# Row maxima of an 8192 x 8192 matrix: first tile in four strided loads, last row by DVE transposes, results in six stores, pieces recut

One core of one Trainium2 chip. The metric is the device time of one execution in microseconds (us), lower is better.

## The reference

```python
x = np.random.randn(8192, 8192).astype(np.float32)
def reference(x):
    return np.linalg.norm(x, ord=np.inf, axis=1)      # max |x| of each row
```

268.4 MB are read and 32 KB are written. 128 rows make a tile, one row to a partition; there are 64 such "rows" of tiles.

## The kernel before

SyncE issues all loads into a ring buffer, most of them for two rows of tiles at once (a double tile). VectorE (DVE) reduces each piece; where a row was cut, a short reduce, called the combine below, puts its partial maxima together. TensorE (PE) and ScalarE (ACT) turn the results round so that each row of results is contiguous, and ACT issues their stores. The last row of tiles is handled apart: its pieces are reduced into columns behind the last piece, and one final reduce takes piece and columns together.

```python
PIECES = (
    [[8192]] * HEAD                       # HEAD = 4
    + [[16384]] * 23                      # two rows of x per partition
    + [[8192, 8192], [7232, 9152], [6720, 9664], [8640, 7744], [5568, 5568, 5248]]
    + [[4480, 3712], [3392, 1920, 2880], [2752, 1600, 2048, 1792]]
    + [[1792, 1664, 1472, 1280, 1088, 896]]
)
RING = 3 * 16384
CUT = 48              # rows below CUT go straight into res, the others through part
...
    fin = single.tile([P, 1], FP32)
...
    def pairs_out():                      # 56 of the 64 rows of results
        ...
        nc.scalar.dma_start(
            out=out[: X_ONE * P].rearrange("(g p r) -> g p r", p=P, r=2), in_=sb)
...
            nc.sync.dma_start(out=buf, in_=src[:, off : off + w])
            if final:
                absmax(fin[:, :1], last)
                break
...
        if u == len(PIECES) - 2:          # all but the last row are reduced
            nc.vector.tensor_reduce(out=res[:, CUT:], in_=part, ...)
            pairs_out()
            singles_out()

    fin_ps = psum_pool.tile([1, P], FP32)
    fin_sb = single.tile([1, P], FP32)
    nc.tensor.transpose(fin_ps, fin, ident)
    nc.vector.tensor_copy(out=fin_sb, in_=fin_ps)
    nc.sync.dma_start(out=out[(R - 1) * P :].rearrange("(r p) -> r p", p=P), in_=fin_sb)
```

No wait is written by hand. The framework adds them, and gives each load and store on SyncE's and ACT's queues one of eight completion semaphores in turn: the issue records name 100, 101 and 103 to 108, seven times each. A semaphore is a counter that a transfer raises as it lands; the seven loads on 100 raised it 112 times.

Of the kernel before, what the change touches and what calls it, by code (L numbers as in the profile page):

```python
# [1 line left out]

# [5 lines left out]

P = 128
FP32 = mybir.dt.float32  # L10
MAX = mybir.AluOpType.max




HEAD = 4
PAIRS = 28
PIECES = (
    [[8192]] * HEAD
    + [[16384]] * 23  # L20
    + [[8192, 8192], [7232, 9152], [6720, 9664], [8640, 7744], [5568, 5568, 5248]]
    + [[4480, 3712], [3392, 1920, 2880], [2752, 1600, 2048, 1792]]
    + [[1792, 1664, 1472, 1280, 1088, 896]]
)
RING = 3 * 16384


CUT = 48
K = 4


@with_exitstack
def kernel(
    ctx: ExitStack,
    tc: tile.TileContext,
    x: bass.AP,
    out: bass.AP,
):
    nc = tc.nc
    n_rows, n_cols = x.shape  # L40
    R = n_rows // P
    assert R == 64 and n_cols == 8192

    X_ONE = 2 * PAIRS

    single = ctx.enter_context(tc.tile_pool(name="single", bufs=1))
    psum_pool = ctx.enter_context(tc.tile_pool(name="psum", bufs=1, space=bass.MemoryType.PSUM))

    ring = single.tile([P, RING], FP32)
    res = single.tile([P, R - 1], FP32)  # L50
    part = single.tile([P, R - 1 - CUT, K], FP32)
    nc.gpsimd.memset(part, 0.0)  # L52
    ident = single.tile([P, P], FP32)
    make_identity(nc, ident)


    n_last = len(PIECES[-1]) - 1
    w_last = PIECES[-1][-1]
    last = single.tile([P, w_last + n_last], FP32)
    fin = single.tile([P, 1], FP32)  # L60

    def absmax(dst, src):
        nc.vector.tensor_reduce(  # L63
            out=dst, in_=src, axis=mybir.AxisListType.X, op=MAX, apply_absolute_value=True,
        )

    def singles_out():
        n = R - 1 - X_ONE
        ps = psum_pool.tile([n, P], FP32, name="ps_singles")
        sb = single.tile([n, P], FP32, name="sb_singles")  # L70
        nc.tensor.transpose(ps, res[:, X_ONE:], ident)  # L71
        nc.scalar.copy(sb, ps)  # L72
        nc.scalar.dma_start(
            out=out[X_ONE * P : (R - 1) * P].rearrange("(r p) -> r p", p=P), in_=sb
        )

    def pairs_out():
        sb = single.tile([PAIRS, P, 2], FP32, name="sb_pairs")
        both = res[:, :X_ONE].rearrange("p (g r) -> p g r", r=2)
        for r in range(2):  # L80
            ps = psum_pool.tile([PAIRS, P], FP32, name=f"ps_pairs{r}")
            nc.tensor.transpose(ps, both[:, :, r], ident)  # L82
            nc.scalar.copy(sb[:, :, r], ps)  # L83
        nc.scalar.dma_start(
            out=out[: X_ONE * P].rearrange("(g p r) -> g p r", p=P, r=2), in_=sb
        )

    at = 0
    next_pair, next_one = 0, X_ONE
    for u, widths in enumerate(PIECES):  # L90
        k = sum(widths) // n_cols
        if k == 2:
            row, next_pair = next_pair, next_pair + 2
        else:
            row, next_one = next_one, next_one + 1
        src = x[row * P : (row + k) * P].rearrange("(p r) m -> p (r m)", r=k)
        off = 0
        n_part = {}
        for h, w in enumerate(widths):
            final = u == len(PIECES) - 1 and h == n_last  # L100
            if final:
                buf = last[:, :w]
            else:
                if at + w > RING:
                    at = 0
                buf = ring[:, at : at + w]
                at += w
            nc.sync.dma_start(out=buf, in_=src[:, off : off + w])  # L108
            if final:
                absmax(fin[:, :1], last)  # L110
                break
            s = 0
            while s < w:
                r = row + (off + s) // n_cols
                left = n_cols - (off + s) % n_cols
                c = (w - s) // n_cols if left == n_cols else 0
                if c and r + c <= CUT:
                    absmax(
                        res[:, r : r + c],
                        buf[:, s : s + c * n_cols].rearrange("p (c m) -> p c m", m=n_cols),  # L120
                    )
                    s += c * n_cols
                    continue
                e = min(w, s + left)
                i = n_part.get(r, 0)
                n_part[r] = i + 1
                if r == R - 1:
                    absmax(last[:, w_last + i : w_last + i + 1], buf[:, s:e])
                else:
                    absmax(part[:, r - CUT, i : i + 1], buf[:, s:e])  # L130
                s = e
            off += w
        if u == len(PIECES) - 2:
            nc.vector.tensor_reduce(  # L134
                out=res[:, CUT:], in_=part, axis=mybir.AxisListType.X, op=MAX,
            )
            pairs_out()
            singles_out()

    fin_ps = psum_pool.tile([1, P], FP32)  # L140
    fin_sb = single.tile([1, P], FP32)
    nc.tensor.transpose(fin_ps, fin, ident)  # L142
    nc.vector.tensor_copy(out=fin_sb, in_=fin_ps)  # L143
    nc.sync.dma_start(out=out[(R - 1) * P :].rearrange("(r p) -> r p", p=P), in_=fin_sb)


# [1 line left out]
_INS = ['x']  # L148
_OUTS = [((8192,), 'float32')]


# [23 lines left out]
```

## Time and profile before

| | before |
|---|---|
| median of 3 runs | 630.57 us (630.52 to 630.62) |
| span of the profiled run | 629.1 us |
| first reduce on DVE starts | 13.30 us |
| last wait of DVE for a load ends | 487.50 us |
| final reduce ends | 626.36 us |

The profile's main views are read in the prediction below. One line more: the waits of DVE for loads. Its columns are the total in us, the number of waits, and the longest. The longest wait is the one for the first tile.

```profile
DVE part L63 <- DMA ring<-in_x_dram: 16.3, 4, 13.3
```

And from the page's groups, the two instructions that bring the last row into one partition (busy us, mean ns of one | idle time before them and what ended it):

```profile
L143 DVE COPY fin_sb<-fin_ps 1x128 f32<-1x128 f32 x1 | 0.3, 279 | 0.5 <-PE fin_ps L142 0.5
...
L142 PE MATMUL fin_ps<-ident,fin 128*1 128x128 f32 x1 | 0.4, 373 | 8.1 <-DVE fin L63 8.1
```

### The profile page before, as it was taken

The page shows a single profiled execution, that of the slowest core. Times are in us where ns is not written, and L with a number is a line of the kernel's source. Part 1 is how long each engine was busy: PE and PEld are TensorE (multiplying, and loading weights), DVE is VectorE, ACT ScalarE, POOL GpSimd, SP SyncE. Part 2 cuts the span into 40 slices and gives each one's busy share as a digit, 9 for nine tenths or more (in the row PEclk, how much of TensorE's full clock was granted, in tenths as well). Part 3 has the DMA queues.
Part 4 walks back from the last instruction along what each step waited for, and adds up shares of the span by engine and source line. Part 5 has one row for each costly group of instructions (what it writes and reads, how often), then busy time and mean ns, then how long its engine had stood idle before and what let it go on. Part 6 is the DMA issues. An engine that isn't in the chain of part 4 may idle for free.

```text
span 629.1 us, 217 instructions
## 1 busy us (share of the span) xinstructions
PE 1.2 (0%) x4; PEld 0.3 (0%) x4; DVE 552.6 (88%) x59; ACT 2.0 (0%) x4; POOL 0.8 (0%) x7
## 2 busy tenths in 40 slices
PE   0000000000000000000000000000000000000000
PEld 0000000000000000000000000000000000000000
DVE  1983988889988889888898888998888999999998
ACT  0000000000000000000000000000000000000000
POOL 0000000000000000000000000000000000000000
DMA  8999999999999999999999999999999999999996
GB/s 367 433 467 404 463 404 463 400 467 404 463 404 463 404 463 404 463 404 463 404 463 404 463 408 458 408 458 408 458 408 429 431 447 432 427 426 424 425 423 265
DMA packets 7692, 268.49 MB, mean 427 GB/s; under 512 B 870, under 2 KB 906, under 8 KB 2058
## 3 DMA queue, kind: packets, MB, share of 16 engines
q1 hardware_dynamic: 7634, 268.44, 99.0%
q10 hardware_dynamic: 56, 0.03, 0.0%
q14 instruction: 2, 0.02, 0.0%
HBM read 268.44 MB, written 0.03 MB: 427 GB/s over the span
## 4 chain that ended last, share of the span: by engine, by line
DMA 57%; DVE 43%; issue 0%; SPq 0%; PE 0%
DMA ring<-in_x_dram 57%; DVE res L63 25%; DVE part L63 17%; DVE last L63 1%; DVE fin L63 0%; SPq L108 0%; PE fin_ps L142 0%; DVE fin_sb L143 0%; DVE res L134 0%
## 5 line engine op out<-in xcount | busy, mean ns | idle before, releaser
L63 DVE TENSOR_REDUCE res<-ring 128x2 f32<-128x16384 f32 (+1 forms) x25 | 413.2, 16536 | 57.6 <-DMA ring<-in_x_dram 57.6
L63 DVE TENSOR_REDUCE part<-ring 128x1 f32<-128x8192 f32 (+19 forms) x26 | 130.0, 5067 | 16.3 <-DMA ring<-in_x_dram 16.3
L63 DVE TENSOR_REDUCE last<-ring 128x1 f32<-128x1792 f32 (+4 forms) x5 | 8.0, 1662 | 0.0
L83 ACT COPY sb_pairs<-ps_pairs 28x128 f32<-28x128 f32 x2 | 0.5, 264 | 615.9 <-PE ps_pairs L82 615.9
L82 PE MATMUL ps_pairs<-ident,res 128*28 128x128 f32 x2 | 0.6, 394 | 617.5 <-DVE res L134 617.5
L83 ACT ACT_TABLE_LOAD x1 | 1.3, 1283 | 0.7 <-PEq L159 0.7
L63 DVE TENSOR_REDUCE fin<-last 128x1 f32<-128x901 f32 x1 | 1.1, 1091 | 0.0
L143 DVE COPY fin_sb<-fin_ps 1x128 f32<-1x128 f32 x1 | 0.3, 279 | 0.5 <-PE fin_ps L142 0.5
L82 PEld LDWEIGHTS ps_pairs<-ident,res 128*28 128x28 f32 x2 | 0.1, 106 | 617.5 <-issue 617.5
L71 PE MATMUL ps_singles<-ident,res 128*7 128x128 f32 x1 | 0.4, 417 | 0.0
L142 PE MATMUL fin_ps<-ident,fin 128*1 128x128 f32 x1 | 0.4, 373 | 8.1 <-DVE fin L63 8.1
masks.py:199 POOL TENSOR_SCALAR_AFFINE_SELECT ident<-ident 128x128 f32<-128x128 f32 x1 | 0.3, 292 | 0.1
L72 ACT COPY sb_singles<-ps_singles 7x128 f32<-7x128 f32 x1 | 0.3, 254 | 0.0
L134 DVE TENSOR_REDUCE res<-part 128x15 f32<-128x60 f32 x1 | 0.2, 216 | 0.0
masks.py:197 POOL MEMSET ident<- 128x128 f32 x1 | 0.2, 204 | 0.0
L52 POOL MEMSET part<- 128x60 f32 x1 | 0.1, 148 | 0.3 <-POOLq L159 0.3
L71 PEld LDWEIGHTS ps_singles<-ident,res 128*7 128x7 f32 x1 | 0.1, 132 | 0.1
L159 POOL MEMSET const-bfloat16-1.0<- 128x1 bf16 x1 | 0.1, 102 | 0.0
L159 POOL MEMSET const-uint8-127<- 128x1 uint8 x1 | 0.1, 102 | 0.0
L159 POOL MEMSET const-float32-0.0<- 128x1 f32 x1 | 0.1, 98 | 0.2 <-issue 0.2
L159 POOL MEMSET const-float32-1.0<- 128x1 f32 x1 | 0.1, 98 | 0.0
L142 PEld LDWEIGHTS fin_ps<-ident,fin 128*1 128x1 f32 x1 | 0.1, 80 | 8.6 <-DVE fin L63 8.6
## 6 DMA issues: line engine op xcount, KB each, us to landing
ring<-in_x_dram SPq DMA_DIRECT2D x6, 4096.0 KB, 21.7
ring<-in_x_dram SPq DMA_DIRECT2D x2, 2784.0 KB, 39.3
ring<-in_x_dram SPq DMA_DIRECT2D x1, 4832.0 KB, 40.7
ring<-in_x_dram SPq DMA_DIRECT2D x1, 4576.0 KB, 40.6
ring<-in_x_dram SPq DMA_DIRECT2D x1, 4320.0 KB, 34.1
ring<-in_x_dram SPq DMA_DIRECT2D x1, 3872.0 KB
ring<-in_x_dram SPq DMA_DIRECT2D x1, 3616.0 KB, 30.1
ring<-in_x_dram SPq DMA_DIRECT2D x1, 3360.0 KB
```

The lines of the kernel that those rows point to most:

```text
L52: nc.gpsimd.memset(part, 0.0)
L63: nc.vector.tensor_reduce(out=dst, in_=src, axis=mybir.AxisListType.X, op=MAX, apply_absolute_value=True,)
L71: nc.tensor.transpose(ps, res[:, X_ONE:], ident)
L72: nc.scalar.copy(sb, ps)
L82: nc.tensor.transpose(ps, both[:, :, r], ident)
L83: nc.scalar.copy(sb[:, :, r], ps)
L134: nc.vector.tensor_reduce(out=res[:, CUT:], in_=part, axis=mybir.AxisListType.X, op=MAX,)
L142: nc.tensor.transpose(fin_ps, fin, ident)
L143: nc.vector.tensor_copy(out=fin_sb, in_=fin_ps)
L159: nc = _bacc.Bacc("TRN2", target_bir_lowering=False, num_devices=1)
```

## The change

Its intent: start all 16 DMA engines sooner with small first loads, store the results in smaller parts, end sooner by leaving out PE and PSUM for the last row, and spend fewer instructions on the pieces near the end. The diff is shortened: `...` and `#` stand for what is left out.

```diff
-    + [[8192, 8192], [7232, 9152], [6720, 9664], [8640, 7744], [5568, 5568, 5248]]
-    + [[4480, 3712], [3392, 1920, 2880], [2752, 1600, 2048, 1792]]
-    + [[1792, 1664, 1472, 1280, 1088, 896]]
+    + [[8192, 8192]] * 3
+    + [[8704, 7680], [6400, 5312, 4672]]
+    + [[4224, 3968], [3328, 2880, 1984], [2496, 2240, 1920, 1536]]
+    + [[1664, 1536, 1472, 1344, 1216, 960]]
-CUT = 48
+CUT = 52
-    fin = single.tile([P, 1], FP32)
+    fin = single.tile([P, 32], FP32)
+    fin_t = single.tile([32, P], FP32)
+    nc.gpsimd.memset(fin, 0.0)
     # pairs_out
-        nc.scalar.dma_start(out=out[: X_ONE * P].rearrange(...), in_=sb)
+        dst = out[: X_ONE * P].rearrange("(g p r) -> g p r", p=P, r=2)
+        cuts = (0, 5, 10, 15, 20, 24, 28)
+        for a, b in zip(cuts, cuts[1:]):
+            nc.scalar.dma_start(out=dst[a:b], in_=sb[a:b])
     # loads
-            nc.sync.dma_start(out=buf, in_=src[:, off : off + w])
+            if u == 0:
+                for first, step in ((0, 8), (4, 8), (2, 4), (1, 2)):
+                    nc.sync.dma_start(out=buf[first::step], in_=src[first::step])
+            else:
+                nc.sync.dma_start(out=buf, in_=src[:, off : off + w])
     # end
-    nc.tensor.transpose(fin_ps, fin, ident)
-    nc.vector.tensor_copy(out=fin_sb, in_=fin_ps)
-    nc.sync.dma_start(..., in_=fin_sb)
+    for q in range(0, P, 32):
+        nc.vector.transpose(fin_t[:, q : q + 32], fin[q : q + 32, :])
+    nc.sync.dma_start(..., in_=fin_t[:1, :])
```

More of the change, by code (lines that the diff above doesn't have):

```diff
@@ L83, in pairs_out @@
             nc.scalar.copy(sb[:, :, r], ps)
-        nc.scalar.dma_start(
-            out=out[: X_ONE * P].rearrange("(g p r) -> g p r", p=P, r=2), in_=sb
-        )
+        dst = out[: X_ONE * P].rearrange("(g p r) -> g p r", p=P, r=2)
+        cuts = (0, 5, 10, 15, 20, 24, 28)
+        for a, b in zip(cuts, cuts[1:]):
+            nc.scalar.dma_start(out=dst[a:b], in_=sb[a:b])
     at = 0
@@ L138 @@
             singles_out()
-    fin_ps = psum_pool.tile([1, P], FP32)
-    fin_sb = single.tile([1, P], FP32)
-    nc.tensor.transpose(fin_ps, fin, ident)
-    nc.vector.tensor_copy(out=fin_sb, in_=fin_ps)
-    nc.sync.dma_start(out=out[(R - 1) * P :].rearrange("(r p) -> r p", p=P), in_=fin_sb)
+    for q in range(0, P, 32):
+        nc.vector.transpose(fin_t[:, q : q + 32], fin[q : q + 32, :])
+    nc.sync.dma_start(out=out[(R - 1) * P :].rearrange("(r p) -> r p", p=P), in_=fin_t[:1, :])
 _INS = ['x']
```

## The prediction

It is on record as it was written, with cuts marked. Rival 1 is that the strided first loads run at half rate. Its factor of two, from which the 2.4 us come, is not shown by the trace before. "The whole of rival 1" is the case of all eight packets of an engine at half rate, 8 x 1.21 = 9.7 us more as an estimate from the packet time. Rival 3 is that the first packets are slow whatever the order. That the bytes forbid a gain of 2% rests on the page of the kernel before: packets take up 99.0% of the 16 engines' span.

> **What bounds the kernel now.** I read the page first, then the chain of work that ended last, then the waits, then windows of the first microseconds, then the groups by form.
>
> ```profile
> PE 1.2 (0%) x4; PEld 0.3 (0%) x4; DVE 552.6 (88%) x59; ACT 2.0 (0%) x4; POOL 0.8 (0%) x7
> ...
> DMA  8999999999999999999999999999999999999996
> GB/s 367 433 467 404 463 404 463 400 467 404 463 404 463 404 463 404 463 404 463 404 463 404 463 408 458 408 458 408 458 408 429 431 447 432 427 426 424 425 423 265
> ...
> HBM read 268.44 MB, written 0.03 MB: 427 GB/s over the span
> ```
>
> The 16 DMA engines are full in every slice but the first and the last. 268.44 MB must be read, so 427 GB/s over the span is nearly all of the time; no part of the change makes these bytes fewer. What can move is the ramp at the start and the part after the last byte. How the two hang together is in the chain:
>
> ```profile
> 429.42 0.02 issue
> 429.44 17.23 DVE res L63
> 446.67 0.02 issue
> 446.69 40.79 DMA ring<-in_x_dram
> 487.48 0.03 issue
> 487.50 34.40 DVE res L63 x3
> 521.90 95.19 DVE part L63 x22
> 617.10 0.02 issue
> 617.12 0.22 DVE res L134
> 617.34 7.91 DVE last L63 x5
> 625.25 0.02 issue
> 625.27 1.10 DVE fin L63
> 626.37 0.04 issue
> 626.41 0.39 PE fin_ps L142
> 626.80 0.02 issue
> 626.83 0.28 DVE fin_sb L143
> ```
>
> Up to 487.50 DVE waits about 2.1 us for every load, so the loads set the pace. From 487.50 to 626.37 DVE has no gap: a load that landed at 487.48 starts it, and from then on its own work is the chain. It is only just behind the loads, though: the last load was issued at 614.48 and took 10.1 us to land, so its data were there at 624.6, while DVE reached it at 625.27. That is 0.7 us of lag. The start:
>
> ```profile
> 1.00:2.00 1.00, 0.00 (x0) 0.00 (x0) 0.00 (x0) 1.00 (x1) 0.31 (x2) 1.00 1.14 295
> 2.00:3.00 1.00, 0.00 (x0) 0.00 (x0) 0.00 (x0) 0.01 (x1) 0.00 (x0) 1.00 0.69 229
> 3.00:4.00 1.00, 0.00 (x0) 0.00 (x0) 0.00 (x0) 0.00 (x0) 0.00 (x0) 1.00 0.84 360
> ```
>
> (The last two columns are DMA share and GB/s.) The first load is issued at 0.74 us; in the packet records the first packets of the 16 engines start between 1.76 and 2.75 us and end between 3.62 and 4.37 us, and those that start early take 2.06 us where every later packet of 32 KB takes 1.21. So the engine that starts worst ends its first packet 1.4 us later than 1.76 + 1.21 = 2.97 us would allow. This lag is never made up: at each landing the last engine is some 0.3 to 0.4 us after the one before it (at the first one 13.20 after 12.91).
>
> [...]
>
> **The change, part by part.**
>
> *Start.* One load of 128 packets becomes four of 16, 16, 32 and 64. [...] If all first packets start at about 1.8 us and take between 1.3 and 2.06 us, they end at 3.1 to 3.85; the worst ended at 4.37, so 0.5 to 1.3 us come off. Issues cost 0.33 to 0.53 us each, less than the 1.21 us of one packet, so engines are not starved between the four, but the fifth load is issued some 1.2 us later than now, still long before 13 us. I take 0.7 us, the lower part[...]. What is gained is carried through the whole run: each load waits for DVE, DVE for a load, and the whole chain up to 487.50 shifts.
>
> *Recut.* From 487.50 on DVE has the same 131,072 columns per partition to reduce (136.53 us at the measured 0.96 columns per ns: 16,384 in 17.07 of 17.22 us). What differs is the number of instructions. Consecutive reduces start 60 ns further apart than their columns need (7,232 columns are 7.53 us; from 521.82 to the next start are 7.59). Before there are 32: one double tile, 2 whole rows, 22 pieces, the combine, 5 and the final one. The new cuts make 30: one, 6, 16, the combine, 5, one, as fewer cuts cross a row and CUT 52 lets two more pairs' rows skip the partial sums. That is 2 x 60 ns, and the combine reads 44 columns for 60 (17 ns): 0.13 us. I put both sets of cuts into a hand-made model (a load takes 0.2946 ns per byte of a partition's row and 50 to 80 ns, as successive landings of the trace show; DVE as above; a load waits for its part of the ring). It ends the final reduce before at 626.39 (the trace: 626.36), and with the new cuts at 626.27, with the last load landing at 624.53 against 624.55. So the last load stays 0.6 to 0.7 us ahead of DVE, and DVE's own work remains the end.
>
> *Row into one partition.* Removed: from the end of the final reduce at 626.36 to the end of the copy at 627.10, that is 0.745 us (matmul 373 ns, copy 279 ns, two hand-overs of about 45 ns). Added: four DVE transposes of 32 columns. The nearest instruction is the combine, 60 columns in 216 ns, so 153 ns fixed; 32 columns make 33 + 153 = 186 ns. Overlapped like the reduces (93 ns apart): 0.035 + 3 x 0.093 + 0.186 = 0.50 us. One after the other[...]: 0.035 + 4 x 0.186 = 0.78 us. I lean to the latter: 0.70, a gain of 0.05. The store and its landing (627.13 to 628.24) are as before. The memset of `fin` lies in POOL's idle time.
>
> *Six stores for one.* They write the same 28 KB while the last row is loading. [...] ACT issues seven stores in some 2 to 3 us from 618.4; they land before 627. Nothing gained.
>
> Sum: 0.70 + 0.13 + 0.05 = 0.88 us; 630.57 - 0.88 = 629.7 us.
>
> **The rivals.**
>
> 1. [...] Then the first two take 2.4 us each for 1.2, a loss of about 2.4 us[...]. [...] Against it: the engines start staggered[...]. 10 to 15%.
>
> 2. *More stores hold up the last loads through completion semaphores.* The issue records show eight of them taken in turn by all loads and stores, and the waits of SyncE's queue say:
>
> ```profile
> SPq L108 <- DMA ring<-in_x_dram: 133.1, 37, 19.8
> ```
>
> 37 times a load's issue waited for an earlier load to land. Now nothing is lost by that, since four or five loads are queued (the third but last load is issued at 609.8 and lands at 622). With seven stores in turn with the last six loads, one of these may have to wait for a store, and the store before landed only at 623. That would make the last load 2 to 4 us late: 632 to 634. The three additional loads and five additional stores make eight, which keeps the turn where it was for whatever follows; I give this 8%.
>
> 3. [...] Then all first packets take 2 us whatever the order, only the worst engine gains, or none: 630.2 to 630.5. For it: 2.06 us for nine engines that started within 0.15 us of each other. Against it: the late ones took 1.27 us beside them. 20%.
>
> 4. *The four transposes are slower than the matmul way.* At 0.25 us each 0.29 us are lost: 630.0.
>
> **Range and chances.** Were start and tail at their best (1.3 + 0.13 + 0.25), 628.9; at rival 3 with slow transposes 630.7. I take 628.7 to 630.9, which leaves rivals 1 and 2 in the upper tail. 2% is 12.6 us: the bytes alone forbid a gain of that size, and only the whole of rival 1 with rival 2 comes near such a loss. Faster 0.01, within 2% 0.97, slower 0.02.
>
> **What would show it.** Start: the first packets of all engines start within about 0.3 us and the first wait of DVE, now 13.30 us, shrinks to about 12.6; a first wait over 14 is rival 1. The 487.50 of the last wait for a load moves by the same amount. Recut: from that landing to the end of the final reduce 138.73 us in place of 138.86, without a gap. Tail: 0.50 to 0.80 us from the final reduce's end to that of the last transpose. A gap on DVE between the last five reduces, or a load issued after 616, would be rival 2. I am wrong altogether if DVE waits for loads again after some 490 us for another reason, as then the lag that hides the stores' share is gone.

## The result, and the profile after

| | before | after | difference |
|---|---|---|---|
| median of 6 runs each | 630.61 us | 635.95 us (635.57 to 636.21) | +5.34 |
| span of the profiled run | 629.1 us | 634.1 us | +5.0 |
| first reduce on DVE starts | 13.30 us | 15.69 us | +2.39 |
| last double tile's reduce starts | 487.50 us | 489.79 us | +2.29 |
| from there to the end of the final reduce | 138.86 us | 141.49 us | +2.63 |
| from there to the end of the last copy or transpose | 0.745 us | 0.875 us | +0.13 |

The ratio is 1.0083 (95% interval 1.0070 to 1.0096); ratios here are the mean time of one kernel's fast runs over that of the other's of the same rounds, so not quite the ratio of the medians quoted. The kernel is 5.3 us slower, within 2% and outside my range. The last three rows of the table add up to 5.05 us: there are two losses of about equal size, one at the start and one near the end, and a small one at the very end.

**The start.** The waits of DVE in the changed kernel, with the same columns as before:

```profile
DVE part L66 <- DMA ring<-in_x_dram: 18.7, 4, 15.7
DVE last L66 <- DMA ring<-in_x_dram: 2.6, 1, 2.6
```

The longest wait, for the first tile, has grown from 13.3 to 15.7 us. The second line is new: DVE waits in the midst of the last row. Windows of 3 us show the rate at the start; the last number of a line is GB/s. First the kernel before, then the changed one:

```profile
4.00:7.00 3.00, 0.00 (x0) 0.00 (x0) 0.00 (x0) 0.00 (x0) 0.00 (x0) 1.00 0.94 404
```

```profile
4.00:7.00 3.00, 0.00 (x0) 0.00 (x0) 0.00 (x0) 0.00 (x0) 0.00 (x0) 1.00 1.02 240
```

The engines are as busy (0.94 and 1.02), yet move 240 GB/s in place of 404. They are not starved: each packet takes longer. A packet here is one row of a tile, 32 KB in the records. These do not name the DMA engine; a packet that starts as another ends is taken for the same engine's, which gives 16 chains of packets in both kernels. The eight packets of 32 KB that each engine carries for the first tile take, in order and as a mean over the engines:

| | 1st | 2nd | 3rd | 4th to 8th |
|---|---|---|---|---|
| before | 1.83 us | 1.22 | 1.21 | 1.21 |
| after | 2.22 us | 2.40 | 1.69 | 1.21 to 1.22 |

The first two loads are one packet per engine each: the 16 packets of the first start between 2.16 and 2.87 us, and none ends before 3.92. The second takes twice the usual time (2.40 us for 1.21). The third load, of two packets per engine, begins slowly: 2.05 us for the engine that comes to it first, 1.40 for the last. These means add up to the loss: the first packets start 0.30 us later (mean), and the first three packets take 0.39, 1.17 and 0.48 us more, 2.34 of the 2.39 us.

**The end.** The chain of work that ended last, in the changed kernel (start us, us, what):

```profile
489.79 68.78 DVE res L66 x7
558.57 60.70 DVE part L66 x16
...
619.30 0.21 DVE res L143
...
620.05 0.48 ACT sb_pairs L86 x2
620.53 0.03 ACT sb_singles L75
620.56 3.72 DMA out_dram<-sb_pairs
624.29 4.29 DMA ring<-in_x_dram
...
628.61 1.43 DVE last L66
...
630.12 1.17 DVE fin L66
...
631.32 0.20 DVE fin_t L150
```

Up to the combine at 619.30 the chain is that of before, 2.18 us later. Then it leaves DVE: it goes through PE and ACT to the store of the pairs' rows, 3.72 us until that has landed at 624.29, and from there to a load that is issued at that moment. Before, the last load had been issued at 614.48. SyncE's queue says the same in its waits:

```profile
SPq L117 <- DMA out_dram<-sb_pairs: 9.1, 1, 9.1
```

A load waited 9.1 us for a store, although no load reads or overwrites what a store handles. The issue records show why. In order, with the semaphore that each takes:

```text
store 5 rows        106      store 5 rows   101
store 5 rows        107      store 4 rows   102
store 5 rows        108      store 4 rows   103
load 1344 columns   100      store singles  104
                             load 1216 columns   106   waits for the first store
                             load  960 columns   107   waits for the second store
```

(105 counts DVE.) Read down the left column, then down the right one. The loads of the last row and the seven stores share eight semaphores in turn. The 1216-column load comes eight places after the first store and needs its semaphore, so it can't be issued before that store has landed: the last landing on 106 is at 624.28 us, the issue at 624.29.

The transposes, from the page's groups:

```profile
L150 DVE STREAM_TRANSPOSE fin_t<-fin 32x32 f32<-32x32 f32 x4 | 0.8, 200 | 0.1
```

### The profile page after: what moved, and what is told of

Same layout as the page of the kernel before. It is cut to its first block, busy times and chain, and to the rows that moved or that the text cites. A ratio compares the mean times of both kernels' runs of the same rounds, so it can differ in the third digit from the quotient of the medians.

```text
span 634.1 us, 228 instructions
## 1 busy us (share of the span) xinstructions
PE 0.8 (0%) x3; PEld 0.3 (0%) x3; DVE 553.1 (87%) x60; ACT 2.0 (0%) x4; POOL 0.8 (0%) x8
## 4 chain that ended last, share of the span: by engine, by line
DMA 58%; DVE 41%; SPq 0%; issue 0%; ACT 0%; PE 0%; DVEq 0%
DMA ring<-in_x_dram 57%; DVE res L66 30%; DVE part L66 11%; DMA out_dram<-sb_pairs 1%; SPq L115 0%; DVE last L66 0%; DVE fin L66 0%; DVE fin_t L150 0%; ACT sb_pairs L86 0%; PE ps_pairs L85 0%; DVEq L177 0%; DVE res L143 0%; DVEq L66 0%; ACT sb_singles L75 0%
## 5 line engine op out<-in xcount | busy, mean ns | idle before, releaser
L66 DVE TENSOR_REDUCE res<-ring 128x2 f32<-128x16384 f32 (+1 forms) x29 | 447.6, 15452 | 57.5 <-DMA ring<-in_x_dram 57.5
L66 DVE TENSOR_REDUCE part<-ring 128x1 f32<-128x8192 f32 (+15 forms) x20 | 95.5, 4837 | 18.7 <-DMA ring<-in_x_dram 18.7
L66 DVE TENSOR_REDUCE last<-ring 128x1 f32<-128x1664 f32 (+4 forms) x5 | 8.0, 1652 | 2.6 <-DMA ring<-in_x_dram 2.6
```

The source lines that it names most:

```text
L66: nc.vector.tensor_reduce(out=dst, in_=src, axis=mybir.AxisListType.X, op=MAX, apply_absolute_value=True,)
```

## The experiments

The theories: the start loses because of which partitions the first loads fill, in the first two every eighth of the 128 (rivals: strided reads from memory, or the cost of more issues); the end loses because of the semaphores (rivals: the traffic of the six stores, the new cuts). All results passed the comparison with the reference. Cuts in the expectations are marked.

### One part undone at a time

`e1_one_store`:

```diff
-        dst = ...
-        cuts = (0, 5, 10, 15, 20, 24, 28)
-        for a, b in zip(cuts, cuts[1:]):
-            nc.scalar.dma_start(out=dst[a:b], in_=sb[a:b])
+        nc.scalar.dma_start(out=out[: X_ONE * P].rearrange(...), in_=sb)
```

> The changed kernel, with the pairs' rows stored in one transfer again (28 rows) in place of six; the four first loads, the new cuts and the transposes stay. Theory (the six stores take six more of the eight completion semaphores in turn, so the last two loads, 1216 and 960 columns, wait for the first two stores to land): the wait of SyncE's queue for a store, 9.1 us in the changed kernel, is gone, the last load is issued by about 617 us and not at 624.7, DVE's 2.6 us gap before the 1216-column reduce is gone, and the time is about 633.0 us (2.9 below the changed kernel, 2.3 above the one before: the start's loss alone). Rival (the stores' traffic or the new cuts make the last loads late, not the semaphores): the gap stays or shrinks by under 1 us; 635 to 636 us.

Measured: 633.60 us (633.51 to 633.81; the kernel before beside it 630.60). SyncE's wait for a store is gone, and so is DVE's gap: from the last double tile to the end of the final reduce it takes 138.80 us (141.49 with six stores). The last load is issued in time, as the timeline shows:

```profile
616.97 0.33 SPq L116 DMA_DIRECT2D last<-in_x_dram  x1
```

The time came out 0.6 us above what I expected. Set against the changed kernel's profile, the last double tile's reduce starts 0.2 us later (489.99), the stretch from there gained 2.7 us where I had counted 2.9, and the time from the last transpose to the end of the program is 0.2 us longer (2.19 against 1.97).

`e2_whole_first`:

```diff
-            if u == 0:
-                for first, step in ((0, 8), (4, 8), (2, 4), (1, 2)):
-                    nc.sync.dma_start(out=buf[first::step], in_=src[first::step])
-            else:
-                nc.sync.dma_start(out=buf, in_=src[:, off : off + w])
+            nc.sync.dma_start(out=buf, in_=src[:, off : off + w])
```

> The changed kernel, with the first tile loaded in one transfer of 128 partitions again; the six stores stay. Theory (the first three of the four loads run at half rate [...], and nothing of that is made up later): DVE's first reduce starts at 13.3 us and not 15.7, its last wait for a double tile ends at 487.5 and not 489.8, and the hold-up by the stores stays as it is (a gap of about 2.6 us on DVE before the 1216-column reduce): about 633.5 us. Rival (the two losses overlap, so that an earlier start only makes the gap at the end longer): 635 to 636 us.

Measured: 633.47 us (633.31 to 633.87). The first reduce starts at 13.15 us, the last double tile's at 487.25. (Of the three slow loads that the theory named, the packet table above shows the second at half rate, and the third slow only at its start.) The gap in the last row stays (2.4 us), and SyncE waits 9.1 us for a store as before. So an earlier start does not lengthen the gap, and the two losses do not hide each other.

`e3_neither` has both edits.

> The changed kernel with both undone: first tile in one transfer and one store for the pairs; what is left of the change is the cuts with CUT 52 and the four transposes. Theory (the two losses add up and are all of it): 630.6 us within 0.3, that is 0.12 us less for two reduces fewer and 0.13 more for the transposes (0.875 us from the final reduce's end to the last transpose's end against 0.745). Rival (the new cuts themselves cost something, or the losses are not independent): over 631.2 us.

Measured: 630.62 us (630.55 to 630.71), the kernel before 630.60; the ratio is 1.0 (0.9984 to 1.0017). With both undone nothing is left of the loss. In this job the start accounts for 633.60 - 630.62 = 2.98 us and the stores for 633.47 - 630.62 = 2.85.

### Why the stores hold the loads up

`e4_stores_gpsimd` keeps the six stores and moves them to a queue that does not draw from the eight semaphores (the issue records show 111 to 116 for them):

```diff
-            nc.scalar.dma_start(out=dst[a:b], in_=sb[a:b])
+            nc.gpsimd.dma_start(out=dst[a:b], in_=sb[a:b])
```

> The changed kernel with its six stores, but issued from GpSimd's queue and not ScalarE's, so that they take no part in the turn of the eight completion semaphores of the loads; same six pieces, same bytes at the same time. Theory (semaphores): the last loads no longer wait for a store, DVE's gap of 2.6 us is gone, about 633.0 us as with one store. Rival (six small stores of 5 or 4 rows [...] hold the loads up by their traffic): the gap stays, 635 to 636 us.

Measured: 633.74 us (633.52 to 633.95), as with one store. The timeline:

```profile
614.81 0.33 SPq L117 DMA_DIRECT2D last<-in_x_dram  x1
620.66 0.56 ACTq L76 DMA_DIRECT2D out_dram<-sb_singles  x1
620.73 3.21 POOL L90 DMA_DIRECT2D out_dram<-sb_pairs  x6 [619.33 <-ACT sb_singles L75]
```

The same six pieces leave from 620.73 on, while the last loads still run, and cost nothing to speak of: 138.96 us from the last double tile to the end of the final reduce, against 138.80 with one store (0.08 of the difference is a wait for a load at 567.56, before any of these stores). It is not their traffic; it is the semaphore that a load has to take after them.

`e5_five_stores` changes the number of stores that stand before the last loads:

```diff
-        cuts = (0, 5, 10, 15, 20, 24, 28)
+        cuts = (0, 6, 12, 18, 24, 28)
```

> The changed kernel with the pairs' rows stored in five transfers (6, 6, 6, 6, 4 rows) in place of six; four first loads stay. Theory (eight semaphores in turn): now only the last load takes a semaphore that a store used (the first one's), and the 1216-column load waits for the third load of the last row to land. So the last load is still issued late, at about 624.4 us, but the 1216-column one earlier, at about 622.7; DVE's gap before the 1216-column reduce shrinks from 2.6 us to about 0.5, and the time is 633.9 to 634.6 us, between the one store's 633.6 and the six stores' 635.95. Rival (the loss grows with the number of small stores as such): about 635.5 us.

Measured: 634.96 us (634.80 to 635.28), 0.4 us above my range and well below the six stores. The waits of DVE, then those of SyncE's queue:

```profile
DVE fin L66 <- DMA last<-in_x_dram: 1.0, 1, 1.0
...
DVE last L66 <- DMA ring<-in_x_dram: 0.5, 1, 0.5
```

```profile
SPq L117 <- DMA out_dram<-sb_pairs: 1.5, 1, 1.5
```

The issues came as worked out from the turn: 1216 columns at 622.79, 960 at 624.62. The gap before the 1216-column reduce is the 0.5 us expected. I had missed a second gap, 1.0 us before the final reduce: the last load took 4.47 us from issue to landing, for 0.49 MB. A third, of 0.35 us, lies earlier: at 567.95 DVE waits for a load that no store held up.

### Why the start is slow

These four kernels are the kernel before with one edit to the first tile's load:

```diff
-            nc.sync.dma_start(out=buf, in_=src[:, off : off + w])
+            if u == 0:
+                ...                       # as below
+            else:
+                nc.sync.dma_start(out=buf, in_=src[:, off : off + w])
# f1_split4          partitions 0::8, 4::8, 2::4, 1::2  <-  the same rows of x
# h1_rows_in_order   partitions 0::8, 4::8, 2::4, 1::2  <-  rows 0:16, 16:32, 32:64, 64:128
# f2_halves_block    partitions 0:64, 64:128            <-  the same rows
# f3_halves_every2   partitions 0::2, 1::2              <-  the same rows
```

> The kernel before with one part of the change alone: the first tile in four loads (every 8th, 8th, 4th and 2nd partition). Theory [...]: the packets of the first two loads take about 2.4 us each where a packet of 32 KB takes 1.21 us later, DVE's first reduce starts at 15.7 to 16.2 us and not 13.3, and the time is 633.0 to 633.6 us (2.4 to 3.0 above the kernel before). Rival (the loss shows only with the new cuts): under 631.5 us.

Measured: 633.44 us (633.37 to 633.65; before 630.67). First reduce at 15.49 us; packets of the first three rounds 2.32, 2.38 and 1.65 us. This part of the change makes the loss by itself, without the new cuts. Not all of its 2.8 us lies at the start: against the first profile of the kernel before, the last double tile's reduce starts 2.1 us later, and in the stretch after it, which takes 139.32 us and not 138.86, DVE waits once more for a load, 0.37 us at 567.99.

> Wrong on purpose in the first tile's 128 results: the same four loads into every 8th, 8th, 4th and 2nd partition, but each reads the next 16, 16, 32 and 64 rows of the input in order, so that the source of each load is one contiguous piece and no longer rows 256 KB apart. Theory (the loss is on the side of the partitions written[...]): unchanged, packets of the first two loads 2.4 us, first reduce at 15.7 to 16.2 us, 633.0 to 633.6 us. Rival (the loss is on the reading side, from rows at a stride of a large power of two): packets of 1.2 to 1.5 us, first reduce at about 13.5 us, 630.6 to 631.2 us.

Measured: 633.38 us (633.37 to 633.48); the second round of packets takes 2.40 us, and the wait for the first tile is

```profile
DVE part L63 <- DMA ring<-in_x_dram: 18.4, 4, 15.4
```

Each load now reads one contiguous piece of memory and is as slow. So the stride of the reads is not the cause. (The comparison with the reference passed in spite of the 128 results in the wrong places; this kernel is of use for its time only.)

> The kernel before with the first tile in two loads of 64 neighbouring partitions each, 0 to 63 and 64 to 127. [...] Theory ([...] each load spread over all 16 engines): all eight packets of each engine take 2.4 us, the first reduce starts near 23 us and the time is near 640 us. Rival A (many short loads cost by their issue[...]): two issues more cheaply made than four, under 631.5 us. Rival B ([...] engines 0 to 7 carry one half and 8 to 15 the other): no packet is slow, about 631 us.

Measured: 641.31 us (641.22 to 641.39), ratio 1.0169. First reduce at 23.82 us. Apart from the first of each half (about 2.2 and 2.4 us), packets take 2.56 us. Windows of this run:

```profile
4.00:7.00 3.00, 0.00 (x0) 0.00 (x0) 0.00 (x0) 0.00 (x0) 0.00 (x0) 1.00 1.07 218
7.00:10.00 3.00, 0.00 (x0) 0.00 (x0) 0.00 (x0) 0.00 (x0) 0.00 (x0) 1.00 1.33 273
```

> The control of the run with neighbouring halves: again two loads of 64 partitions, but the even and the odd ones[...]. Theory [...]: packets of 1.21 us after the first, first reduce at 13.2 to 13.8 us, 630.5 to 631.1 us. Rival (strided partitions or the second issue cost the time): a start as late as with four loads, 633 us.

Measured: 630.95 us (630.89 to 631.06), ratio 1.0005 (0.9988 to 1.0022). First reduce at 13.38 us. The same windows:

```profile
4.00:7.00 3.00, 0.00 (x0) 0.00 (x0) 0.00 (x0) 0.00 (x0) 0.00 (x0) 1.00 1.22 524
7.00:10.00 3.00, 0.00 (x0) 0.00 (x0) 0.00 (x0) 0.00 (x0) 0.00 (x0) 1.00 0.81 350
```

A packet is counted in these windows in one piece, so single windows swing; over the six microseconds the halves of neighbours move (218 + 273) / 2 = 246 GB/s and the halves of every second partition (524 + 350) / 2 = 437. The number of issues, their sizes and the bytes are the same. What differs is which partitions each load fills, and which rows it reads, which the run with the rows in order has shown not to be the cause; that is worth 10.4 us. Rivals A and B fall with the first half of this pair, the cost of issues with the second.

### Trying for a faster kernel

`g1_direct` stores the 128 last maxima as they lie, one per partition:

```diff
-    nc.tensor.transpose(fin_ps, fin, ident)
-    nc.vector.tensor_copy(out=fin_sb, in_=fin_ps)
-    nc.sync.dma_start(out=out[(R - 1) * P :].rearrange("(r p) -> r p", p=P), in_=fin_sb)
+    nc.sync.dma_start(out=out[(R - 1) * P :].rearrange("(p r) -> p r", r=1), in_=fin)
```

> The kernel before without any move of the last row into one partition: the 128 maxima are stored as they lie, one 4-byte piece per partition. It tries for a kernel faster than both. Theory (the 0.745 us of matmul and copy lie wholly on the path of the end, and 128 pieces of 4 bytes over 16 DMA engines take little longer than one of 512 bytes, as completion packets of 4 bytes take 9 ns): the store is issued at about 626.4 us and not 627.1, and the time is 629.9 to 630.2 us. Rival (small pieces land late): the store takes 0.7 us or more longer to land, 630.6 us or above.

Measured: 636.41 us (635.60 to 636.57; before 630.74), a clear miss. SyncE's last wait, for the store to land, in the kernel before and in this one:

```profile
SPq L170 <- DMA out_dram<-fin_sb: 0.5, 1, 0.5
```

```profile
SPq L166 <- DMA out_dram<-fin: 6.4, 1, 6.4
```

The store is issued 0.03 us after the final reduce, as intended. Its 128 packets are all taken up by 626.96 us, 7 to 9 ns each (nearly all packets of 4 bytes in the kernel before take 9), but their completions arrive from 629.3 to 633.0. So the packets' times in the record do not show when this store was confirmed: 7.06 us after its issue began (625.93 to 632.995), where the one piece of 512 bytes in the kernel before took 1.11 (627.13 to 628.24). Why is not shown.

`g2_recut_alone` is the kernel before with the new `PIECES` and `CUT = 52`.

> The kernel before with the new cuts and CUT 52 alone. Theory (two reduces fewer at 60 ns, 16 columns fewer in the combine): from the landing that starts DVE's last unbroken stretch to the end of the final reduce 138.73 us in place of 138.86, 630.4 to 630.6 us. Rival (cuts move the last load's landing): over 630.8 us.

Measured: 630.87 us (630.75 to 631.13), ratio 1.0003 (0.9991 to 1.0016): no difference that these runs resolve. From the last double tile to the end of the final reduce it took 138.91 us, not 138.73. The trace shows where the gain went: up to the combine the 0.11 us are there (129.51 against 129.62), but the load of 1216 columns lands only at 623.55, DVE has caught up with it and starts that reduce at 623.58, and from the combine on it takes 9.40 us. With the same cuts in `e3_neither` that load lands just in time (623.24, reduce at 623.27), and the part takes 9.28.

`g3_recut_direct` has both.

> New cuts and direct store of the 128 maxima together, on the kernel before. Theory: the two gains add, 629.8 to 630.1 us, which would be the fastest of all. Rival: as for the direct store alone, 630.5 us or above.

Measured: 636.24 us (635.80 to 636.50), as the direct store alone. No version beat the kernel before; the one with both losses undone equals it.

## Why the prediction was wrong

**The start: the step that failed.** I took 0.7 us off, on first packets that "start at about 1.8 us and take between 1.3 and 2.06 us". Neither half of this holds. The first packets start later, between 2.16 and 2.87 us after the change against 1.76 to 2.75 before, in part since the issue of the 16-row load takes 0.63 us and that of the 128-row load 0.40. (I had put issues at 0.33 to 0.53 us and the next tile's load 1.2 us later; it is issued 2.1 us later, at 3.31 for 1.20.) And the first packets are slow however short the first load is: 2.22 us as a mean with 16 rows, 1.88 even with interleaved halves, 1.83 with 128 rows, against 1.21 later. In the kernels that load the first tile at once, only the engines that start after 2.5 us take 1.21 to 1.37. This is what the third rival, which I gave 20%, expected of the times; what makes the first packets slow is not shown. On top came the first rival, at 10 to 15%: two loads at half rate for "a loss of about 2.4 us". Its sum comes out by some luck: the two loads cost 1.6 us more (0.39 and 1.17), the rest is the third load and the later start. In the profiles the first reduce of the kernels with four loads starts 2.1 to 2.9 us later than in those with one. The trace before has no load that fills only some of the partitions, so it could not show half rate, and I let that count for the change. The pair of halves shows it: in the windows from 4 to 22 us the 16 engines are as busy with 64 neighbouring partitions as with every second one (mean DMA share 1.00 and 1.01), and move 208 GB/s in place of 437.

**The stores: the second step that failed.** I expected them to "land before 627. Nothing gained", and gave the hold-up 8%. They did land before 627, the last at 625.04; what failed is that nothing would wait for them. The 8% rested on the argument that three more loads and five more stores "make eight, which keeps the turn where it was". That is the wrong sum. What counts is how many loads and stores stand between a store and a later load: when the distance is eight, the load waits for the store. The size I named for the rival, 2 to 4 us, was right (2.6 us in DVE's gap, 2.85 in time). The sign to look for, "a load issued after 616", is what the profile shows: 624.66.

**The recut: right up to the combine, without effect.** From the last double tile to the start of the combine the changed kernel takes 129.50 us and the one before 129.62 (619.30 - 489.79 and 617.12 - 487.50, rounded after subtraction of the exact starts): the 0.12 us worked out. By itself it gained nothing that the runs resolve. My model had the last load 0.6 to 0.7 us ahead of DVE; in `g2_recut_alone` it lands 0.3 us before the final reduce, and the load before it 0.02 us before its own, which cost the 0.12 us again. I had looked at the last load alone.

**The tail: mis-sized.** I took 0.70 us for the transposes; they take 0.875. One transpose takes 199 ns, not 186, and they start 213 ns apart, so each starts only after the one before it has ended. What makes them wait is not shown. I had leaned to one after the other and then taken less than its 0.78. In place of a gain of 0.05 us there is a loss of 0.13.

**What stays open.** The single losses in one job, 2.98 and 2.85, add up to 0.5 us more than the changed kernel lost against the same base in another job (635.95 - 630.62 = 5.33). The profiled runs show the same difference, 5.83 us in sum against 5.35: a start that differs from run to run accounts for 0.3 us of it (first reduce at 15.39 to 15.86 us in the six kernels with these four loads) and the time from the last transpose to the end for 0.4 (2.19 and 2.16 us in `e1_one_store` and `e2_whole_first`, 1.97 in the changed one and in `e3_neither`, though the last store lands 1.10 to 1.11 us after its issue in all four), less 0.2 for the gap on DVE. Why these differ no run shows. Nor do the runs say why shorter loads take longer to issue (the first loads of 16 to 64 rows 0.56 to 0.63 us, a first load of 128 rows 0.38 to 0.40), or why the third load begins slowly. And they do not say why blocks of 64 and every eighth partition are slow beside every second one: which engine fills which partition is not recorded.

## What to carry to other kernels

Before cutting a load by partitions, measure the pieces: here every second partition ran at full rate (1.21 us a packet), while blocks of 64 (2.56) and every eighth partition (2.33 to 2.40) ran at about half. Where a framework gives out a small number of completion semaphores in turn (eight here, and a load waited 9.1 us for a store), count the transfers between a store that ends late and the loads after it, and keep few stores ahead of the last loads, or issue them from a queue with semaphores of its own. And a stage that only costs a fraction of a microsecond, like bringing 128 values into one partition, may be what spares several microseconds of tiny writes (here 0.745 us beside 7.06 for 128 pieces of 4 bytes and 1.11 for one of 512 bytes).
